# Two transposes of the first attention head leave TensorE for VectorE and a round trip through HBM

## The chip, the cores and the metric

The kernel runs on one core of one Trainium2 chip. The metric is the device time of one execution in microseconds (us). Before the change it is 1411.34 us, the median of three runs (1411.06 to 1411.61).

The core's engines each work through a queue of their own, in order: TensorE (PE; its weight loads are listed apart as PEld), VectorE (DVE), ScalarE (ACT), GpSimd (POOL), and SyncE (SP), which here only issues DMAs. An engine waits when the instruction at the head of its queue waits.

## The reference

Two layers, 512 tokens, width 1024, float32. Cut to what matters here:

```python
for i in range(DEPTH):                                   # 2
    xn = rmsnorm(x, norm1_g[i])
    u_pool, q, k, v, g_a, g_b = split(xn @ w_in[i])
    q, k = rotary(rmsnorm(q)), rotary(rmsnorm(k))        # 4 heads x 2 halves x 128
    p = softmax(where(chunk_causal, q @ k.T * scale, neg))
    a = p[:, :, 0] - lam * p[:, :, 1]                    # one probability matrix per head
    o = rmsnorm(a @ v, subln_g[i]) * (1.0 - lam_init)    # v: 256 wide per head
    merged = sigmoid(g_a) * pool_mixer(u_pool) + sigmoid(g_b) * o
    x = x + merged @ w_out[i]
    x = x + (silu(gate) * up) @ w_ffn_out[i]             # gate, up = split(rmsnorm(x) @ w_ffn_in[i])
```

## The kernel before, in words

Every float32 product is done as three products of rounded halves: `split` (L196) makes a high part on ACT (a cast) and a low part on DVE (a subtraction), and `product` (L277) issues high x high, high x low, low x high on PE. So a tile that PE is to use passes through ACT and DVE first, and its low part is the last to be ready.

The four heads are processed in the order 3, 2, 1, 0. Below, the first (number 3 of the first layer) is called A and the second B. Tokens are in four tiles t = 0 to 3 of 128. For each head `attention` (L549) does this:

- For each tile a product gives q and k (512 wide); ACT squares them with sums, DVE and POOL make the reciprocal root `r` (L328, L329), DVE scales (L659) and rotates (L431), and `qn` is the result. It is transposed, split into `qh`, `ql` (L198, L199) and used by `scores` (L569).
- `scores` computes two score tiles `sc` of (t+1) x 128 columns, takes the maximum on DVE, the exponential on ACT, and combines both halves into `prob[0]` on DVE (L587).
- The probabilities must be transposed before they can be multiplied with v. `turn_prob` (L595) splits the transposed tile into `ah` and `al`.
- `weighted` (L609) multiplies with v into a PSUM tile (`oy`, and for A's odd tiles one of the two score tiles `sc`), normalises and gates it on DVE into `m` (tile `mt`, L617 to L620).
- `turn_out` (L628) puts the transposed `m` into `mj`, which the merge of this head (`merged`, L724) adds much later.

A transpose is done in one of two ways. `transpose` (L302) is a PE instruction with an identity, 128x128, into PSUM. `turned` (L306) transposes 32x32 squares on DVE into `near` (L310), writes `near` to HBM (`away`, L311) and reads it back in four DMAs with the squares in their new places (L313); SP issues all five, and each read waits for the write to land. `near` shares its buffers with the tiles it is made from: `pr0`/`pr1` for probabilities, `mt` for outputs.

Before the change A uses PE for all its transposes (qn, probabilities, outputs), and so do the last head's outputs. All other heads' qn and probabilities, and the outputs of B and of the third head, go by `turned`.

The order of the work is set twice. The code keeps a clock of PE work (`clock`, counted in columns of a product, so one unit is about 0.44 us per thousand) and a list of steps due later (`later`, L263; `run_due`, L267): the delays of L47 and L49 say how much PE work lies between a step and the next. A step that `need` (L337) asks for is run early. A scheduler then places each instruction in its engine's queue by its own estimate of durations, so neighbouring steps can be interleaved.

Weights are loaded by SP into seven buffers (`raw`), in the order in which they are used, and split into six pairs (`whi`, `wlo`).

Of the kernel before, what the change touches and what calls it, by code (L numbers as in the profile page):

```python
# [18 lines left out]
P = 128  # L19
# [3 lines left out]
NT = S // P  # L23
# [19 lines left out]
ORDER = (3, 2, 1, 0)  # L43

HIDDEN_AT = {0: "u", 2: "m", 4: "pr", 6: "us", 8: "mj", 10: "u", 12: "m", 14: "pr", 16: "us", 18: "u", 20: "m"}

SCORE_WAIT, PROB_WAIT, AV_WAIT, NORM_WAIT, MERGE_WAIT = 33600, 25200, 11400, 15000, 15000  # L47

QK_AWAY, SCORE_AWAY, PROB_AWAY, MERGE_AWAY = 28000, 26000, 32000, 24000  # L49

# [59 lines left out]
def trunk_kernel(  # L110
# [21 lines left out]
    def s_ps():  # L132
        return ps.tile([P, 512], F32, name="sc", tag="sc", bufs=2)

    def tr_ps():
        return ps.tile([P, 512], F32, name="tr", tag="tr", bufs=2)
# [59 lines left out]
    def split(hi, lo, src):  # L196

        ins = nc.scalar.copy(hi, src)  # L198
        nc.vector.tensor_sub(lo, src, hi.bitcast(F32))  # L199
        return ins  # L200
# [62 lines left out]
    def later(delay, what):  # L263
        heapq.heappush(waiting, (clock[0] + delay, count[0], what))
        count[0] += 1
# [11 lines left out]
    def product(acc, pairs):  # L277

        n = len(pairs)
        for i, ((ah, al), (bh, bl)) in enumerate(pairs):  # L280
            run_due()
            nc.tensor.matmul(acc, lhsT=ah, rhs=bh, start=i == 0, stop=False)  # L282
            nc.tensor.matmul(acc, lhsT=ah, rhs=bl, start=False, stop=False)  # L283
            nc.tensor.matmul(acc, lhsT=al, rhs=bh, start=False, stop=i == n - 1)  # L284
            clock[0] += 3 * acc.shape[-1]
# [16 lines left out]
    def transpose(dst, src):  # L302
        nc.tensor.transpose(dst, src, ident)  # L303
        clock[0] += 2 * P

    def turned(src, n, tag, bufs):  # L306

        near = sb.tile([P, n * P], F32, name="near", tag=tag, bufs=bufs)
        away = hbm.tile([P, n * P], F32, name="away", tag="away", bufs=8)
        nc.vector.transpose(near.rearrange("p (c k j) -> p k c j", c=4, k=n), src.rearrange("p (k c i) -> p k c i", k=n, c=4))  # L310
        nc.sync.dma_start(away, near)  # L311
        for c in range(4):
            nc.sync.dma_start(  # L313
                near[32 * c:32 * (c + 1), :].rearrange("i (q r) -> i q r", q=4),
                away.rearrange("(q i) (c r) -> c i q r", q=4, c=4)[c])
        return near.rearrange("p (q k j) -> p k q j", q=4, k=n)

    def squares_of(x):
        return x.rearrange("p k (q j) -> p k q j", q=4)
# [12 lines left out]
    def small(name, width=1):  # L332
        return sb.tile([P, width], F32, name=name, tag=name, bufs=4)
# [109 lines left out]
    def token(t):  # L443
        return slice(t * P, (t + 1) * P)
# [90 lines left out]
    for layer in range(L):  # L535
# [13 lines left out]
        def attention(j, before, then):  # L549
# [9 lines left out]
            def turn(t, qn):  # L559
                if at_start:  # L560
                    tp = tr_ps()
                    for h in range(4):
                        transpose(tp[:, h * P:(h + 1) * P], qn[:, h, :])
                    split(qh[:, :, token(t)], ql[:, :, token(t)], tp.rearrange("p (h c) -> p h c", h=4))
                else:
                    split(squares_of(qh[:, :, token(t)]), squares_of(ql[:, :, token(t)]), qn)
                later(SCORE_WAIT if at_start else SCORE_AWAY, lambda: scores(t))

            def scores(t):  # L569
                width = (t + 1) * P  # L570
                prob = []
                st = small("st", 2)
                mx = small("mx", 2)
                for c in range(2):
                    sc = s_ps()
                    product(sc[:, :width], [(
                        (qh[:, c, token(t)], ql[:, c, token(t)]), (qh[:, 2 + c, :width], ql[:, 2 + c, :width]))])
                    nc.vector.memset(sc[:CHUNK, width - CHUNK:width], MASKED)
                    nc.vector.tensor_reduce(mx[:, c:c + 1], sc[:, :width], axis=AX.X, op=ALU.max, negate=True)
                    pr = sb.tile([P, S], F32, name="pr", tag=f"pr{c}", bufs=2)  # L580
                    nc.scalar.activation(pr[:, :width], sc[:, :width], AF.Exp, bias=mx[:, c:c + 1], accum_out=st[:, c:c + 1])
                    prob.append(pr[:, :width])
                rc = small("rc", 2)
                nc.vector.reciprocal(rc, st)
                nc.vector.tensor_mul(rc[:, 1:2], rc[:, 1:2], neglam[layer])
                nc.vector.tensor_scalar_mul(prob[1], prob[1], rc[:, 1:2])
                nc.vector.scalar_tensor_tensor(prob[0], prob[0], rc[:, 0:1], prob[1], op0=ALU.mult, op1=ALU.add)  # L587
                if at_start:
                    later(PROB_WAIT + (4000 if t == NT - 1 else 0), lambda: turn_prob(t, prob[0]))
                else:  # L590
                    near = turned(prob[0], t + 1, f"pr{t % 2}", 2)
                    later(PROB_AWAY, lambda: turn_prob(t, near))
                ready.add((layer, j, "s", t))

            def turn_prob(t, pr):  # L595
                if at_start:
                    tp = tr_ps()
                    for k in range(t + 1):
                        transpose(tp[:, token(k)], pr[:, token(k)])
                apart = at_start and t % 2  # L600
                ah, al = (sb.tile([P, S], F32R, name="a" + p, tag="u" if apart else "a" + p, bufs=2 if apart else 1) for p in "hl")
                width = (t + 1) * P
                if at_start:
                    split(ah[:, :width], al[:, :width], tp[:, :width])
                else:
                    split(*(squares_of(x[:, :width].rearrange("p (k c) -> p k c", c=P)) for x in (ah, al)), pr)
                later(AV_WAIT, lambda: weighted(t, ah, al))

            def weighted(t, ah, al):  # L609
                if (layer, j, "v", t) not in ready:  # L610
                    later(2400, lambda: weighted(t, ah, al))
                    return
                o = s_ps()[:, :VD] if at_start and t % 2 else o_ps()
                product(o, [((ah[:, token(k)], al[:, token(k)]), (v_at(vh, k), v_at(vl, k))) for k in range(t + 1)])
                ss = small("sso")
                m = sb.tile([P, VD], F32, name="mt", tag="mt", bufs=3)
                nc.scalar.activation(m, o, AF.Square, accum_out=ss)  # L617
                r = rsqrt_mean(ss, VD, 1, (1.0 - lam_init,))
                nc.vector.scalar_tensor_tensor(m, o, r, sg[layer], op0=ALU.mult, op1=ALU.mult)
                nc.vector.scalar_tensor_tensor(m, tb[t // 2][:, t % 2, :], 1.0, m, op0=ALU.add, op1=ALU.mult)  # L620
                ready.add((layer, j, "o", t))
                if near_end:
                    later(MERGE_WAIT, lambda: turn_out(t, m))
                else:
                    near = turned(m, 2, "mt", 3)
                    later(MERGE_AWAY, lambda: turn_out(t, near))
# [9 lines left out]
                ready.add((layer, j, "mj", t))  # L636

            at_start = not layer and j == ORDER[0]
            near_end = at_start or j == ORDER[-1]
            if not at_start:  # L640
                w = wblock(KD)
            for t in range(NT):
# [298 lines left out]
        for i, j in enumerate(ORDER):  # L941
            then = (lambda: project_out(ORDER[i - 2:i - 1], False)) if i >= 2 else None
            mjs[j] = attention(j, ORDER[i - 1] if i else None, then)
            if i:
                mix(i - 1)
# [102 lines left out]
```

## Time and profile before

| | us |
|---|---|
| median of 3 runs | 1411.34 |
| the profiled execution | 1411.17 |
| its span in the profile | 1409.4 |
| PE transposes of A's probabilities | 10, from 56.0 to 71.7 |
| PE transposes of A's outputs | 8, from 69.8 to 85.9 |

The page of the profile gives each engine's busy time and count, then the chain of work that ended last, followed back from the end. The view of waits says who waited for whom (us in total, times, longest). The view of stretches gives each engine's busy time between two moments. The timeline lists instructions with start, length, engine, line, tiles and the idle time ahead of them. All times are us from the start of the span.

### The profile page before, as it was taken

How to read it: one execution, taken by the hardware profiler on the slowest of the kernel's cores; microseconds unless marked ns; L12 is line 12 of the kernel's file. 1: busy time of each engine (PE TensorE's matmuls, PEld its weight loads, DVE VectorE, ACT ScalarE, POOL GpSimd, SP SyncE). 2: the span in 40 equal slices, each digit the busy share in tenths (PEclk: the TensorE clock that was granted, in tenths of full speed). 3: DMA queues.
4: the chain of work that ended last, by engine and by line, in shares of the span. 5: the costliest groups of instructions: out<-in, count | busy, mean ns of one | idle time of the engine just before them, and what ended most of it. 6: DMA issues, size and time to landing. Idle time of an engine off the chain costs nothing.

```text
span 1409.4 us, 21870 instructions
## 1 busy us (share of the span) xinstructions
PE 1403.4 (100%) x8156; PEld 1239.0 (88%) x8156; DVE 1023.0 (73%) x1915; ACT 686.8 (49%) x1309; POOL 118.2 (8%) x144
## 2 busy tenths in 40 slices
PE   9999999999999999999999999999999999999999
PEld 7888888888999899989888888888889998999897
DVE  7779787687998548737578787767769975676462
ACT  6554343443766346526354543435447662563350
POOL 1010000100001001000010101000010000010000
PEclk9999999999999999999999999999999999999999
DMA  9345353443278357629335355434424682685351
GB/s 363 104 130 148 121 164 108 141 147 84 75 180 208 111 132 183 190 49 235 120 115 170 117 168 166 142 112 154 145 45 120 161 231 73 150 185 160 99 141 60
DMA packets 104219, 201.11 MB, mean 143 GB/s; under 512 B 32688, under 2 KB 56752, under 8 KB 104112
## 3 DMA queue, kind: packets, MB, share of 16 engines
q1 hardware_dynamic: 94176, 166.14, 36.6%
q0 software_dynamic: 8640, 31.46, 12.6%
q10 hardware_dynamic: 1296, 2.11, 0.5%
q8 instruction: 64, 1.05, 0.3%
q14 instruction: 43, 0.35, 0.1%
HBM read 183.02 MB, written 16.65 MB: 142 GB/s over the span
## 4 chain that ended last, share of the span: by engine, by line
PE 95%; DVE 2%; DMA 1%; issue 0%; POOL 0%; ACT 0%; SPq 0%; DVEq 0%; POOLq 0%; ACTq 0%
PE mm L282 19%; PE mm L284 19%; PE mm L283 19%; PE mm L296 6%; PE mm L297 6%; PE mm L294 6%; PE sc L294 3%; PE sc L297 3%; PE sc L296 3%; PE tr L297 1%; PE tr L296 1%; PE tr L294 1%; PE tr L303 1%; PE sc L284 1%; PE sc L283 1%; PE sc L282 1%
## 5 line engine op out<-in xcount | busy, mean ns | idle before, releaser
L198 ACT CAST whi<-raw 128x1024 fp32r<-128x1024 f32 (+1 forms) x225 | 234.6, 1047 | 212.6 <-issue 92.9
L199 DVE TENSOR_TENSOR wlo<-raw,whi 128x1024 fp32r<-128x1024 f32 (+1 forms) x225 | 271.8, 1215 | 74.2 <-ACT whi L198 71.5
L282 PE MATMUL mm<-whi,xh 128*128 128x512 f32 x480 | 188.7, 393 | 0.0
L283 PE MATMUL mm<-wlo,xh 128*128 128x512 f32 x480 | 187.2, 390 | 0.0
L284 PE MATMUL mm<-whi,xl 128*128 128x512 f32 x480 | 187.2, 390 | 0.0
L761 DVE TENSOR_TENSOR res<-mm,res 128x512 f32<-128x512 f32 (+1 forms) x97 | 65.7, 682 | 113.2 <-PE mm L284 113.2
L284 PE MATMUL mm<-whi,fl 128*128 128x512 f32 (+1 forms) x358 | 138.5, 387 | 0.0
L282 PE MATMUL mm<-whi,fh 128*128 128x512 f32 (+1 forms) x358 | 138.3, 387 | 0.0
L283 PE MATMUL mm<-wlo,fh 128*128 128x512 f32 (+1 forms) x358 | 138.2, 387 | 0.0
L329 POOL TENSOR_TENSOR r<-r,mhalf 128x1 f32<-128x1 f32 (+1 forms) x76 | 63.8, 840 | 614.5 <-DVE r L328 493.5
L284 PEld LDWEIGHTS mm<-whi,xl 128*128 128x128 f32 x480 | 90.1, 188 | 19.2
L283 PEld LDWEIGHTS mm<-wlo,xh 128*128 128x128 f32 x480 | 90.3, 188 | 17.4
L282 PEld LDWEIGHTS mm<-whi,xh 128*128 128x128 f32 x480 | 90.2, 188 | 17.4
L238 POOL DMA_DIRECT2D wlo<-in_wts x60 | 52.6, 876 | 604.3 <-ACT wlo L237 290.4
L282 PE MATMUL mm<-xh,whi 128*128 128x512 f32 x256 | 100.4, 392 | 0.0
L283 PE MATMUL mm<-xl,whi 128*128 128x512 f32 x256 | 99.8, 390 | 0.0
L284 PE MATMUL mm<-xh,wlo 128*128 128x512 f32 x256 | 99.8, 390 | 0.0
L296 PE MATMUL mm<-xql,whi 128*128 128x256 f32 x352 | 99.7, 283 | 0.0
L294 PE MATMUL mm<-xqh,whi 128*128 128x256 f32 x352 | 99.6, 283 | 0.0
L297 PE MATMUL mm<-xqh,wlo 128*128 128x256 f32 x352 | 99.6, 283 | 0.0
L294 PE MATMUL sc<-xqh,whi 128*128 128x256 f32 x320 | 90.7, 283 | 0.0
L294 PE MATMUL mm<-xrh,whi 128*128 128x256 f32 x320 | 90.6, 283 | 0.0
(243 smaller groups left out, 3512.1 us busy)
## 6 DMA issues: line engine op xcount, KB each, us to landing
raw<-in_wts SPq DMA_DIRECT2D x244, 512.0 KB, 4.3
wlo<-in_wts POOLq DMA_DIRECT2D x60, 512.0 KB, 7.6
away<-near SPq DMA_DIRECT2D x35, 256.0 KB, 2.4
near<-away SPq DMA_DIRECT2D x140, 64.0 KB, 2.1
away<-near SPq DMA_DIRECT2D x27, 128.0 KB, 1.8
near<-away SPq DMA_DIRECT2D x108, 32.0 KB, 2.3
xr<-in_x_t SPq DMA_DIRECT2D x4, 512.0 KB, 7.0
res<-in_x SPq DMA_DIRECT2D x4, 512.0 KB, 9.0
```

The costliest lines, as they stand in the source:

```text
L198: ins = nc.scalar.copy(hi, src)
L199: nc.vector.tensor_sub(lo, src, hi.bitcast(F32))
L238: nc.gpsimd.dma_start(lo.rearrange("p a b -> p (a b)"), wts[piece_no], accum_op=ALU.add)
L282: nc.tensor.matmul(acc, lhsT=ah, rhs=bh, start=i == 0, stop=False)
L283: nc.tensor.matmul(acc, lhsT=ah, rhs=bl, start=False, stop=False)
L284: nc.tensor.matmul(acc, lhsT=al, rhs=bh, start=False, stop=i == n - 1)
L294: nc.tensor.matmul(acc[:, i, :], lhsT=ah, rhs=bh, start=start and not i and not k, stop=False, skip_group_check=True)
L296: nc.tensor.matmul(acc[:, i, :], lhsT=ah, rhs=bl, start=False, stop=False, skip_group_check=True)
L297: last = nc.tensor.matmul(acc[:, i, :], lhsT=al, rhs=bh, start=False, stop=i == 1 and k == 3, skip_group_check=True)
L303: nc.tensor.transpose(dst, src, ident)
L329: nc.gpsimd.tensor_tensor(r, r, mhalf[:, :width], op=ALU.pow)
L761: added = nc.vector.tensor_add(res[t][:, cs], here, res[t][:, cs])
```

## The change

A's probabilities and outputs now go by `turned`, like those of B. Only its q and k are still transposed by PE. The delay `PROB_WAIT` falls away: for A the step from probabilities to `turn_prob` is now 32000 units (`PROB_AWAY`) instead of 25200 (29200 for the last tile), and from `m` to `turn_out` 24000 (`MERGE_AWAY`) instead of 15000.

```diff
-SCORE_WAIT, PROB_WAIT, AV_WAIT, NORM_WAIT, MERGE_WAIT = 33600, 25200, 11400, 15000, 15000
+SCORE_WAIT, AV_WAIT, NORM_WAIT, MERGE_WAIT = 33600, 11400, 15000, 15000
...
-                if at_start:
-                    later(PROB_WAIT + (4000 if t == NT - 1 else 0), lambda: turn_prob(t, prob[0]))
-                else:
-                    near = turned(prob[0], t + 1, f"pr{t % 2}", 2)
-                    later(PROB_AWAY, lambda: turn_prob(t, near))
+                near = turned(prob[0], t + 1, f"pr{t % 2}", 2)
+                later(PROB_AWAY, lambda: turn_prob(t, near))
...
             def turn_prob(t, pr):
-                if at_start:
-                    tp = tr_ps()
-                    for k in range(t + 1):
-                        transpose(tp[:, token(k)], pr[:, token(k)])
...
-                if at_start:
-                    split(ah[:, :width], al[:, :width], tp[:, :width])
-                else:
-                    split(*(squares_of(x[:, :width].rearrange("p (k c) -> p k c", c=P)) for x in (ah, al)), pr)
+                split(*(squares_of(x[:, :width].rearrange("p (k c) -> p k c", c=P)) for x in (ah, al)), pr)
...
-            near_end = at_start or j == ORDER[-1]
+            near_end = j == ORDER[-1]
```

What this moves in the queues is seen in three places. (Lines from 588 on are ten lower in the changed kernel, and the number behind a tile's name tells the instances of one program apart; `xh`, `xl` are the input's halves.)

PE, where A's last tile is weighted. Before, `mm_849` is B's third q/k product, `mt_807` an output tile of A, `sc_903` the weighted sum of A's fourth tile with `ah_858`, `al_859`:

```order
L282 MATMUL mm_849<-whi_694,xh_118 128x512
L283 MATMUL mm_849<-wlo_695,xh_118 128x512
L284 MATMUL mm_849<-whi_694,xl_119 128x512
L303 MATMUL tr_899<-ident_68,mt_807 128x128 x2
L282 MATMUL sc_903<-vh_381,ah_858 128x256
L283 MATMUL sc_903<-vl_382,ah_858 128x256
L284 MATMUL sc_903<-vh_381,al_859 128x256
```

Now `mm_942` is B's fourth q/k product (the third, `mm_857`, has ended ahead of it), `sc_976` the weighted sum of A's fourth tile with `ah_877`, `al_878`:

```order
L282 MATMUL mm_942<-whi_712,xh_118 128x512
L283 MATMUL mm_942<-wlo_713,xh_118 128x512
L284 MATMUL mm_942<-whi_712,xl_119 128x512
L282 MATMUL mm_942<-whi_718,xh_118 128x512
L282 MATMUL sc_976<-vh_381,ah_877 128x256
L283 MATMUL sc_976<-vl_382,ah_877 128x256
L283 MATMUL mm_942<-wlo_719,xh_118 128x512
L284 MATMUL mm_942<-whi_718,xl_119 128x512
L284 MATMUL sc_976<-vh_381,al_878 128x256
```

The sum has moved from inside B's third product into its fourth, and the transposes around it are gone.

DVE, around the low part of the same tile. Before, `r_827` and `qn_821` belong to B's second tile, `mt_807` to A's second output:

```order
L328 TENSOR_SCALAR r_809<-sso_806 128x1
L619 SCALAR_TENSOR_TENSOR mt_807<-sc_799,r_809,hg_234 128x256
L620 SCALAR_TENSOR_TENSOR mt_807<-tb_383,mt_807 128x256
L328 TENSOR_SCALAR r_827<-ss4_822,stats_70 128x2 x2
L659 SCALAR_TENSOR_TENSOR qn_821<-mm_762,r_827,hg_234 128x128 x4
L199 TENSOR_TENSOR al_859<-tr_853,ah_858 128x512
```

Now `qn_829` belongs to B's second tile, `mt_889` to A's second output, `r_920` and `qn_914` to B's third tile, `wlo_1072` to weights that B needs later:

```order
L328 TENSOR_SCALAR r_891<-sso_888 128x1
L310 STREAM_TRANSPOSE near_849<-qn_829 128x4x4x32
L609 SCALAR_TENSOR_TENSOR mt_889<-sc_881,r_891,hg_234 128x256
L610 SCALAR_TENSOR_TENSOR mt_889<-tb_383,mt_889 128x256
L310 STREAM_TRANSPOSE near_896<-mt_889 128x2x4x32
L328 TENSOR_SCALAR r_920<-ss4_915,stats_70 128x2 x2
L649 SCALAR_TENSOR_TENSOR qn_914<-mm_857,r_920,hg_234 128x128 x4
L199 TENSOR_TENSOR wlo_1072<-raw_1069,whi_1071 128x1024
L199 TENSOR_TENSOR al_878<-near_693,ah_877 128x512
```

The low part has moved behind the third tile's `r` and `qn` and behind a weight split.

SP, from A's first trip on. Before, thirteen weight loads stand in a row here and the trips of B's q and k follow them:

```order
L212 DMA raw<-in_wts 128x1024 x9
L311 DMA away<-near 128x128
L313 DMA near<-away 32x4x32 x4
L212 DMA raw<-in_wts 128x1024 x3
L311 DMA away<-near 128x256
L313 DMA near<-away 32x4x64 x4
L311 DMA away<-near 128x384
L212 DMA raw<-in_wts 128x1024
L313 DMA near<-away 32x4x96 x4
```

The trips of A's probabilities (128 to 512 wide) now stand between the weight loads; further on, up to four writes stand ahead of the first read. Past A's and B's stretch the queues hold the same instructions in the same order on PE.

## The prediction

> **What bounds the kernel now.** I read the page from the busy times to the chain that ended last, then the waits of TensorE, then the stretches in which the first two heads run.
>
> ```profile
> PE 1403.4 (100%) x8156; PEld 1239.0 (88%) x8156; DVE 1023.0 (73%) x1915; ACT 686.8 (49%) x1309; POOL 118.2 (8%) x144
> PE 95%; DVE 2%; DMA 1%; issue 0%; POOL 0%; ACT 0%; SPq 0%; DVEq 0%; POOLq 0%; ACTq 0%
> PE mm L456 <- DVE cold L449: 1.2, 1, 1.2
> PE oy L284 <- DVE al L199: 0.5, 2, 0.4
> PE tr L512 <- DVE xh L499: 0.4, 1, 0.4
> PE oy L282 <- ACT ah L198: 0.2, 1, 0.2
> ```
>
> TensorE (PE) is busy without a gap, it makes 95% of the chain, and in the whole span it waits 2.3 us for anybody (the four rows of its waits: total, times, longest). So an instruction taken off PE is worth what it holds PE for, and any wait put on PE costs its full length.
>
> ```profile
> 60.00:75.00 15.00, 15.00 (x81) 12.64 (x80) 10.65 (x35) 6.55 (x29) 3.58 (x4) 1.00 0.23 79
> 75.00:90.00 15.00, 15.00 (x79) 12.63 (x79) 12.07 (x33) 9.28 (x29) 2.12 (x4) 1.00 0.36 111
> 105.00:120.00 15.00, 15.00 (x72) 12.64 (x71) 13.96 (x30) 8.67 (x20) 0.55 (x1) 1.00 0.50 151
> 120.00:135.00 15.00, 14.62 (x75) 12.32 (x73) 14.01 (x40) 5.95 (x12) 1.92 (x2) 1.00 0.35 104
> ```
>
> The columns of these stretches are PE, weight load, VectorE (DVE), ACT, POOL, granted clock, DMA share, GB/s. The clock is full. DVE is the engine behind PE: 11 to 12 of 15 us busy where the first head (A) hands over to the second (B), 14 of 15 us in B's stretch, where PE already waits 0.4 us for a DVE result (`al`, in 120 to 135).
>
> **What goes.** Ten transposes of A's probabilities (1+2+3+4) and eight of its outputs (4 tiles of 2).
>
> ```profile
> L303 PE MATMUL tr<-ident,pr x10: 270/271/273, 56.0 to 71.7; 128*128 128x128 f32 x10
> L303 PE MATMUL tr<-ident,mt x8: 271/272/273, 69.8 to 85.9; 128*128 128x128 f32 x8
> 71.12 0.39 PE L284 MATMUL mm<-whi,xl 128*128 128x512 f32 x1
> 71.35 0.60 PE L303 MATMUL tr<-ident,pr 128*128 128x128 f32 x4
> 71.70 0.47 PE L282 MATMUL mm<-whi,xh 128*128 128x512 f32 x1
> 72.02 0.39 PE L283 MATMUL mm<-wlo,xh 128*128 128x512 f32 x1
> ```
>
> One lasts 0.27 us but they overlap, so the price is read from starts. Between the start of the four and the second product behind them lie 72.02 - 71.35 = 0.67 us; the product alone takes 0.23 (71.12 to 71.35). Four cost 0.44, one 0.11. Eighteen: **-1.98 us**. [...] The trace shows 0.27 as the length of one and 0.11 as its distance to the next, and PE pays the distance.
>
> **What comes.** Eight DVE square transposes, eight writes to HBM and 32 reads back, all issued by SP, and longer delays before the work that needs them.
>
> ```profile
> L310 DVE STREAM_TRANSPOSE near<-pr x4: 313/506/709, 96.6 to 120.6; 128x128 f32<-128x128 f32 x1, 128x256 f32<-128x256 f32 x1, 128x384 f32<-128x384 f32 x1, 128x512 f32<-128x512 f32 x1
> L310 DVE STREAM_TRANSPOSE near<-mt x4: 435/438/439, 114.1 to 138.3; 128x256 f32<-128x256 f32 x4
> 71.03 0.33 SPq L311 DMA_DIRECT2D away<-near  x1
> 73.06 2.02 SPq L313 DMA_DIRECT2D near<-away  x4
> near<-away SPq DMA_DIRECT2D x4, 64.0 KB, 2.1
> near<-away SPq DMA_DIRECT2D x4, 16.0 KB, 2.0
> ```
>
> Head B has the same four shapes now, so every piece has a price: on DVE 4 x 0.51 for the probabilities and 4 x 0.44 for the outputs, 3.8 us by durations (about 3.2 by starts), spread over 49 to 96 us. On SP one trip is 2.0 us from the write to the first read, 2.0 of issuing, and 2.1 (last two rows, by size) to the last landing: about 6.2 us. Cover for DVE: it idles 4.4 and 2.9 us in the stretches 60 to 75 and 75 to 90. None of this is on the chain by itself.
>
> The reads of A's narrow tiles come in pieces of 128 or 256 bytes. [...] In the rows above the 16 KB reads of B's first tile, in pieces of 128 bytes, land as soon as the 64 KB ones. Were they twice as slow, the first tile would be some 2 us later and cost PE under 1 us by the next paragraph.
>
> Past which queue work is moved: on SP the 13 weight loads in a row are cut after the ninth by the first trip.
>
> ```profile
> 52.59 0.33 SPq L212 DMA_DIRECT2D raw<-in_wts  x1
> 85.26 1.05 ACT L198 CAST whi<-raw 128x1024 fp32r<-128x1024 f32 x1 [0.20 <-PE mm L284]
> ```
>
> The tenth of these loads is issued at 52.59 and its cast is at 85.26. Counted in order it is the eighth cast from 50 us on. A load that starts 4 us later is still some 25 us early, so I cost this at nothing; were that cover gone, it would cost the whole delay.
>
> First tile of A: its weighted sum now needs a trip instead of one transpose. Its softmax ends on DVE at 49.46 (first row below), the transpose at 49.8, and the trip of 6.2 us, less a little for a small write, lands near 55.5. Behind its cast (0.3) ACT has a weight cast (1.05) and a tanh (0.5), up to 57.3, and then the exponential on which the fourth tile's scores wait:
>
> ```profile
> 49.11 0.35 DVE L587 SCALAR_TENSOR_TENSOR pr<-pr,rc 128x128 f32<-128x128 f32 x1
> 57.92 0.58 ACT L581 ACTIVATE pr<-sc,mx 128x384 f32<-128x384 f32 x1 [0.23 <-DVE mx L579]
> 58.65 0.50 PE L282 MATMUL sc<-qh 128*128 128x512 f32 x1
> ```
>
> The exponential runs about 0.4 later (DVE has one more transpose ahead), PE comes there 0.5 later as well, since three more products stand ahead. Bounds: 0 to 0.8 us of wait; I take 0.
>
> **The wait I expect: A's fourth tile.** In the new order of DVE its low part `al` stands behind B's third tile (r, qn) and a weight split; before it stood behind B's second tile.
>
> ```profile
> 72.62 0.35 DVE L328 TENSOR_SCALAR r<-ss,stats 128x2 f32<-128x2 f32 x2
> 74.17 1.13 DVE L659 SCALAR_TENSOR_TENSOR qn<-mm,r,hg 128x128 f32<-128x128 f32 x4 [1.20 <-POOL r L329]
> 75.22 0.68 DVE L199 TENSOR_TENSOR al<-tr,ah 128x512 fp32r<-128x512 f32 x1
> 77.00 0.38 PE L303 MATMUL tr<-ident,mt 128*128 128x128 f32 x2
> 77.13 0.36 PE L282 MATMUL sc<-vh,ah 128*128 128x256 f32 x1
> 78.64 0.40 PE L282 MATMUL mm<-whi,xh 128*128 128x512 f32 x1
> 79.53 0.28 ACT L655 ACTIVATE qn<-mm 128x128 f32<-128x128 f32 x1 [0.22 <-PE mm L284]
> 80.46 0.22 ACT L655 ACTIVATION_READ_ACCUMULATOR qn<-mm 128x1 f32 x1
> 81.64 0.35 DVE L328 TENSOR_SCALAR r<-ss,stats 128x2 f32<-128x2 f32 x2
> 83.18 1.13 DVE L659 SCALAR_TENSOR_TENSOR qn<-mm,r,hg 128x128 f32<-128x128 f32 x4 [1.19 <-POOL r L329]
> 84.23 1.22 DVE L199 TENSOR_TENSOR wlo<-raw,whi 128x1024 fp32r<-128x1024 f32 x1
> 85.36 0.29 DVE L436 TENSOR_TENSOR m<-qn,tab 128x128 f32<-128x128 f32 x1
> ```
>
> Now `al` is done near 75.8 and PE needs it near 77.4. Afterwards: B's third product ends on PE at 79.31 before (0.22 ahead of ACT's square). Ahead of it go away ten probability transposes (1.12 with 0.02 of switching), four of the outputs (0.44), and the weighted sums of A's third and fourth tile, which move behind it (12 products from 77.13 to 78.64 are 1.51, nine 1.1): 75.1. From there PE runs 6 products of B's fourth tile (1.37), the third weighted sum (1.08), 7 more products (1.60), two of the fourth sum (0.24), two more (0.46), and wants `al` at **79.9**. DVE: ACT's four squares end 0.22 + 1.15 behind 75.1, so r can start at 76.5; but ahead of it stand two transposes and the first half of an output tile. Laid end to end from the second tile's qn (PE gives its product near 68.8) they free DVE at 76.9. Then r to qn 1.55 (rows, twice), qn 1.05, the weight split 1.13, `al` 0.6: **81.3**. PE waits **1.4 us**. If DVE is free when r is ready it is 0.8; if POOL or the trips make DVE 0.9 later it is 2.2. I keep 0.7 and 2.2 as ends.
>
> **What follows in B.** Everything behind that wait shifts with PE. In B's stretch DVE has one us in 15 free, and its order there is new too.
>
> ```profile
> 132.31 0.65 DVE L199 TENSOR_TENSOR al<-near,ah 128x512 fp32r<-128x512 f32 x1
> ```
>
> Laying DVE's rows end to end from B's scores I get `al` of B's four tiles between 0.4 and 0.6 us before PE wants them, the last at about 137.3 against 137.7. The old wait of 0.4 (for the row above) may go or stay; I count nothing for it, with ends of -0.4 and +2. Later heads keep their order.
>
> **Sum** against the profiled execution's 1411.17 us (span 1409.4 and 1.8 around it; the median is 0.17 higher, less than this sum can tell): 1411.17 - 1.98 + 1.4 = **1410.6 us**.
>
> **Rivals.**
> 1. *The gain arrives whole.* `al` would have to be done by 79.9, so DVE would have to reach B's third tile before its squares end and the weight split would have to overlap. For it: the waits of before are tiny. Against it: r to `al` alone is 4.3 us behind a product that PE ends 4.75 us before its need, with 1.4 of squares between. Time 1411.17 - 1.98 = 1409.2, with the old wait gone 1408.8.
> 2. *Slower: DVE becomes the bound in B.* Place: 105 to 140 us. There DVE is 28 of 30 us busy; the 3.2 us of new transposes must be absorbed before, in the 7.3 us it idles between 60 and 90. Those idles are waits for POOL and ACT in the middle of chains, so perhaps they can't be filled. If none is absorbed, and SP's trips, of which up to four writes now stand ahead of the first read, add one more landing of 2.1, PE waits 1.4 + 3.2 + 2.1: 1411.17 - 1.98 + 6.7 = 1415.9. It decides once DVE is over 0.5 late in B, and makes the kernel measurably slower from 4.8 us of waits in all. Half of it gives 1412.5.
> 3. *The change doesn't take PE's work away.* The order lists no such transposes for A any more; nothing speaks for it.
>
> **How the numbers follow.** This kernel's measurement can tell about 0.2%, 2.8 us, from no change. Forecast (wait 0.7 to 2.2): 0.50. Rival 1: 0.20, no change by that bound. Half of rival 2, up to 1414: 0.15. Rival 2 in full: 0.12. More than 2.8 us faster needs a gain that I can't find on PE: 0.03. So faster 0.03, same 0.85, slower 0.12. The range leaves out rival 2 in full and the tip of rival 1: 1408.9 to 1413.6.
>
> **What would show it.** PE with 18 transposes fewer; a new PE wait of 0.7 to 2.2 us for `al` near 80 us (a weighted sum in the scores' buffer); no PE wait for weights; trips of 6 to 7 us. Wrong would be: no wait there (rival 1), waits of several us between 100 and 140 us for `al`, `ql` or `ul` (rival 2), or a wait for the exponentials near 59 us.

## The result and the profile after

| | before | after |
|---|---|---|
| median of 22 runs, us | 1411.39 | 1413.7 |
| lowest to highest | 1410.85 to 1412.17 | 1412.83 to 1415.39 |
| the profiled execution, us | 1411.17 | 1413.29 |
| its span | 1409.4 | 1411.5 |

The ratio is 1.0016 with a 95% interval of 1.001 to 1.0023: the changed kernel is 2.3 us slower, where 0.6 us faster was forecast. Two single runs of experiments 6 and 9 with a far lower granted clock (0.66 and 0.89; 1976 and 2679 us) are left out of every figure below. The page's busy times and the first line of its chain, after:

```profile
PE 1403.0 (99%) x8138; PEld 1236.9 (88%) x8138; DVE 1025.0 (73%) x1923; ACT 686.5 (49%) x1309; POOL 117.4 (8%) x144
PE 93%; DVE 3%; DMA 2%; SPq 1%; issue 1%; ACT 0%; POOL 0%; DVEq 0%; ACTq 0%; POOLq 0%
```

The 18 transposes are gone from PE (8156 to 8138) and eight are new on DVE (1915 to 1923). The chain now leaves PE for DMA, DVE and SP. The waits of PE over the whole span (total, times, longest), after:

```profile
PE sc L284 <- DVE al L199: 1.7, 1, 1.7
PE mm L456 <- DVE cold L449: 1.2, 1, 1.2
PE oy L284 <- DVE al L199: 1.1, 2, 0.7
PE sc L282 <- ACT pr L581: 0.6, 1, 0.6
PE oy L282 <- ACT ah L198: 0.2, 1, 0.2
PE sc L282 <- ACT ah L198: 0.2, 1, 0.2
```

2.3 us of waits became 5.0. Three rows are new, the first, the fourth and the sixth; the third grew from 0.5, and a wait of 0.4 for `xh` is gone. The stretches in which the large ones of A and B lie, after:

```profile
75.00:90.00 15.00, 13.10 (x67) 10.64 (x66) 12.81 (x30) 7.20 (x19) 3.71 (x4) 1.00 0.39 117
90.00:105.00 15.00, 14.36 (x71) 12.03 (x70) 10.40 (x37) 6.08 (x23) 1.01 (x1) 1.00 0.41 131
105.00:120.00 15.00, 15.00 (x69) 12.32 (x68) 11.53 (x24) 9.66 (x21) 0.54 (x1) 1.00 0.31 85
120.00:135.00 15.00, 15.00 (x74) 12.57 (x74) 14.50 (x40) 5.27 (x13) 1.32 (x2) 1.00 0.58 183
```

PE has holes of 1.9 us in 75 to 90 and 0.6 in 90 to 105, and none from 105 to 135; the hole of 0.4 that stood in the last row before is gone.

**A's fourth tile, near 82 us.** SP, ACT, DVE and PE of the changed kernel (the two SP rows first, with the number of DMAs; then ACT; then DVE; then PE):

```profile
69.09 2.94 SPq L311 DMA_DIRECT2D away<-near  x3
72.14 6.91 SPq L313 DMA_DIRECT2D near<-away  x12
76.44 0.28 ACT L645 ACTIVATE qn<-mm 128x128 f32<-128x128 f32 x1 [2.74 <-DVE near L310]
78.77 0.64 ACT L198 CAST ah<-near 128x512 fp32r<-128x512 f32 x1
77.37 0.45 DVE L310 STREAM_TRANSPOSE near<-mt 128x256 f32<-128x256 f32 x1
77.74 0.32 DVE L328 TENSOR_SCALAR r<-ss,stats 128x2 f32<-128x2 f32 x2
79.26 1.13 DVE L649 SCALAR_TENSOR_TENSOR qn<-mm,r,hg 128x128 f32<-128x128 f32 x4 [1.20 <-POOL r L329]
80.30 1.22 DVE L199 TENSOR_TENSOR wlo<-raw,whi 128x1024 fp32r<-128x1024 f32 x1
81.43 0.69 DVE L199 TENSOR_TENSOR al<-near,ah 128x512 fp32r<-128x512 f32 x1
79.46 0.39 PE L282 MATMUL sc<-vh,ah 128*128 128x256 f32 x1 [0.16 <-ACT ah L198]
80.03 0.40 PE L284 MATMUL mm<-whi,xl 128*128 128x512 f32 x1
82.17 0.38 PE L284 MATMUL sc<-vh,al 128*128 128x256 f32 x1 [1.74 <-DVE al L199]
```

This is the forecast wait, in the forecast place, with the forecast line in front of it (r, qn, a weight split, `al`). PE could have gone on at 80.03 + 0.23 = 80.26 and went on at 82.17, so 1.91 us are lost here; with the small wait for `ah` ahead of it about 2.2. The trip was not what held it up. Its write was issued at 69.09, and the last of its four reads (the first four of the twelve) was issued at 73.53 and took 3.1 us, so the data had landed near 76.6, after 7.5 us where 6 to 7 were forecast. `ah` was cast 2.2 us later, because ACT had the squares of B's third tile, a weight cast and an output's square ahead of it without a gap. Those squares had begun only at 76.44, though PE had finished their product near 75.1: by the profile, DVE's transpose of B's second tile released them. So ACT's line put off `ah`, and the late squares put off r as well as DVE's own line did (they ended near 77.6, r began at 77.74).

**B's second tile of scores, near 97 us.** DVE, then PE:

```profile
96.17 0.71 DVE L310 STREAM_TRANSPOSE near<-qn 128x512 f32<-128x512 f32 x1
96.81 0.25 DVE L579 TENSOR_REDUCE mx<-sc 128x1 f32<-128x128 f32 x1
97.60 0.39 PE L282 MATMUL sc<-qh 128*128 128x256 f32 x1 [0.64 <-ACT pr L581]
```

There are two score tiles. The second one comes free only when ACT has taken the exponential of what it held before, for which DVE must find the maximum, and DVE is late: it gets to this maximum at 96.81, behind a transpose, though PE had made those scores by 91.8. The prediction had looked for B's waits at `al`, not here.

**The third head, near 216 us.** The same product in the trace of before and, in the second fence, of after:

```profile
214.03 0.40 PE L283 MATMUL mm<-xl,whi 128*128 128x512 f32 x1
214.58 0.38 PE L284 MATMUL oy<-vh,al 128*128 128x256 f32 x1
```

```profile
216.45 0.38 PE L284 MATMUL oy<-vh,al 128*128 128x256 f32 x1 [0.73 <-DVE al L199]
```

The product ahead of it starts at 215.32, so PE loses 0.90 us here, where it lost 0.32 before.

How the loss adds up is read from PE's own position. The first product of A's merge and the first one that reads `fh`, before and then after:

```profile
145.21 0.39 PE L282 MATMUL mm<-whi,mh 128*128 128x512 f32 x1
466.06 0.40 PE L282 MATMUL mm<-whi,fh 128*128 128x512 f32 x1
```

```profile
146.14 0.39 PE L282 MATMUL mm<-whi,mh 128*128 128x512 f32 x1
467.94 0.40 PE L282 MATMUL mm<-whi,fh 128*128 128x512 f32 x1
```

By the end of B the change has cost 0.93 us net of its gain, by 466 us 1.88, and the span ends 2.1 later. So about half of the net loss arises behind both heads that the change touches (0.7 to 1.1 us between these two products in the six profiles of the changed kernel).

### The profile page after: what moved, and what is told of

The parts are those of the page before. It is cut to its first block, busy times and chain, and to the rows that moved or that the text cites. A ratio compares the mean times of both kernels' runs of the same rounds, so it can differ in the third digit from the quotient of the medians.

```text
span 1411.5 us, 21911 instructions
## 1 busy us (share of the span) xinstructions
PE 1403.0 (99%) x8138; PEld 1236.9 (88%) x8138; DVE 1025.0 (73%) x1923; ACT 686.5 (49%) x1309; POOL 117.4 (8%) x144
## 4 chain that ended last, share of the span: by engine, by line
PE 93%; DVE 3%; DMA 2%; SPq 1%; issue 1%; ACT 0%; POOL 0%; DVEq 0%; ACTq 0%; POOLq 0%
PE mm L283 18%; PE mm L282 18%; PE mm L284 18%; PE mm L296 6%; PE mm L294 6%; PE mm L297 6%; PE sc L294 3%; PE sc L297 3%; PE sc L296 3%; PE tr L297 1%; PE tr L296 1%; PE tr L294 1%; DMA near<-away 1%; PE tr L303 1%; SPq L313 1%
```

## The experiments

The times of the kernel before, taken alongside, are 1411.19 for experiments 1 to 4, 1411.10 for 5 to 8 and 1411.21 for 9. The theory at the start: the wait near 82 us is the largest loss, the third head's the second. The rivals: the gain was never there; the loss belongs to the outputs' half; or DVE is late as a whole and any wait that is taken away comes back at its next customer.

**1. What a transpose on PE is worth.** The kernel before, each of the 18 transposes issued twice:

```
 transpose(tp[:, token(k)], pr[:, token(k)])
+nc.tensor.transpose(tp[:, token(k)], pr[:, token(k)], ident)
...
+nc.tensor.transpose(tp[:, a * P:(a + 1) * P], m[:, a * P:(a + 1) * P], ident)
```

> The kernel before, with each of the 18 transposes of the first head's probabilities and outputs issued twice in a row on TensorE; the second writes the same place with the same values, and nothing else is changed. It prices one transpose in place. Theory A (the prediction's price, 0.11 us each, the start-to-start spacing): 18 x 0.11 = 2.0 us slower than before, near 1413.4 us. Rival B (the rows' duration counts, 0.27 each): 4.9 us slower, near 1416.3. Rival C (TensorE's time there is not on the path): no change, 1411.4.

Measured 1412.94 (1412.71 to 1413.34) against 1411.19: +1.75 us, 0.10 for one. Theory A. PE pays the distance between starts, not the 0.27 us that a row shows, and the gain forecast was right within 0.23 us.

**2. The weighted sum of the fourth tile later.** The changed kernel with

```
-later(AV_WAIT, lambda: weighted(t, ah, al))
+later(AV_WAIT + (8000 if at_start and t == NT - 1 else 0), lambda: weighted(t, ah, al))
```

> The changed kernel, with the weighted sum of the first head's fourth tile due 8000 later in the planner's units, so that TensorE takes it up behind the second head's fourth projection and not in the middle of it. VectorE's order ahead of `al` stays. Theory A (most of the loss is the wait for `al` of the fourth tile near 82 us, 2.4 us by start spacings): that wait goes, and the time is 1.8 to 2.6 us below the changed kernel's, near 1411.5. Rival B (the wait only moves to the next place where VectorE is late, the second head's scores or its `al`): the wait near 82 goes and the waits behind it grow by as much, 1413.7. Rival C (the loss comes from SP's order of weight loads and trips in the third head): the time falls by the wait near 82 at most and the third head keeps its wait of 0.7 us near 216.

Measured 1413.4 (1412.21 to 1414.72). The wait for `al` near 82 is gone, and this stands in the waits of 54 to 146 us:

```profile
PE sc L282 <- DVE mt L609: 2.1, 1, 2.1
```

The sum uses one of the two score tiles, and B's scores now wait for DVE to empty it. Rival B; the wait in the third head stays too (0.8), as rival C had it.

**3 and 4. Each half alone.** The outputs alone are the kernel before with the first pair of lines, the probabilities alone the changed kernel with the second:

```
-near_end = at_start or j == ORDER[-1]
+near_end = j == ORDER[-1]
...
-near_end = j == ORDER[-1]
+near_end = at_start or j == ORDER[-1]
```

> Half of the change: the first head's four output tiles go by VectorE's squares and the trip through HBM, its probabilities stay on TensorE (8 transposes fewer than before, not 18). Theory A (the cost is that `al` of the fourth tile stands behind a longer line on VectorE and a trip, so it belongs to the probabilities): 8 x 0.11 = 0.9 us faster than before, 1410.5, and no TensorE wait for `al` near 80 us. Rival B (SP's order in the third head costs about 0.9 and comes with the outputs' trips): no change against before, 1411.4, with a wait of 0.7 near 216. Rival C (VectorE's time as such costs): slower than before by about a quarter of the changed kernel's loss, 1412.

> The other half: the first head's probabilities go by VectorE's squares and the trip, its four output tiles stay on TensorE (10 transposes fewer than before). Theory A (the cost belongs to the probabilities): a TensorE wait for `al` of the fourth tile of 0.5 to 2 us near 80, and 10 x 0.11 = 1.1 us gained against it: between 1411.0 and 1413. Rival B (the cost belongs to the outputs' trips): no wait for `al` near 80 and 1.1 us faster than before, 1410.3.

Outputs alone: 1412.72 (1411.89 to 1413.71), +1.5 us. Probabilities alone: 1411.73 (1411.49 to 1412.54), +0.5, inside what can be told from no change. (The profile of the latter is of its slowest run.) Together 2.0, near the whole. The wait for `al` does belong to the probabilities, as the waits of that run between 54 and 146 us have it:

```profile
PE sc L284 <- DVE al L199: 1.3, 1, 1.3
```

but ten transposes saved (1.0) pay for most of it. The outputs' half costs more although it has no such wait (0.4 us for an earlier tile, 0.6 in the third head). Of that run's theories C comes nearest in the time, but the wait of 0.6 near 216 is the one that rival B named. PE shows where the loss lies: at A's merge this kernel stands at 145.30 against 145.21, its gain used up, at the first `fh` product at 466.66 against 466.06, and its span is 1.4 us longer. So nearly all of its net loss lies behind B.

**5 and 6. The outputs' half taken apart.** The kernel before, with PE's transposes left in, plus either the four square transposes on DVE, whose result nothing reads, or the four trips, whose result nothing reads; both into tiles of the buffers `mt` that the change uses, and both for A alone (`if at_start`, left out below).

```
+near = sb.tile([P, VD], F32, name="near", tag="mt", bufs=3)
+nc.vector.transpose(near.rearrange("p (c k j) -> p k c j", c=4, k=2), m.rearrange("p (k c i) -> p k c i", k=2, c=4))
```

```
+scr = sb.tile([P, VD], F32, name="near", tag="mt", bufs=3)
+away = hbm.tile([P, VD], F32, name="away", tag="away", bufs=8)
+nc.sync.dma_start(away, m)
+for c in range(4):
+    nc.sync.dma_start(
+        scr[32 * c:32 * (c + 1), :].rearrange("i (q r) -> i q r", q=4),
+        away.rearrange("(q i) (c r) -> c i q r", q=4, c=4)[c])
```

> The kernel before, plus the four square transposes of the first head's output tiles on VectorE, into a tile from the outputs' own buffers that nothing reads; no trip is made, TensorE still transposes. It adds 4 x 0.45 = 1.8 us of VectorE alone. Theory A (VectorE's time and place in line cost): TensorE's waits for `al` and for the score buffers grow, 0.5 to 1.5 us slower than before, 1411.7 to 1412.7. Rival B (the loss of the outputs' half comes from the trips on SP): no change, 1411.2.

> The kernel before, plus the four trips of the first head's output tiles through HBM (one write, four reads each) into tiles of the outputs' buffers that nothing reads; no square transposes on VectorE, TensorE still transposes, so nothing waits for what the trips bring. Theory A (VectorE is the cost): no change, 1411.2. Rival B (the trips push other trips and weight loads back on SP, also in later heads): 1 to 2.4 us slower than before, 1412.2 to 1413.6, with a wider spread of the single times as in the outputs-only kernel (1411.89 to 1413.71).

DVE's part: 1411.88, +0.8, which can't be told from no change (1411.5 to 1413.0; five of the eleven times are 1412.4 or more). The trips' part: 1414.57, +3.5, with nobody waiting for what they bring. This is two groups of times: four runs with a clock of 1.0 at 1413.0 (+1.9, in the range of rival B) and six with a clock of 0.998 or 0.999 at 1414.5 to 1414.9 (experiment 10 tells of this clock). Rival B holds in the price, not in the mechanism: the third head loses only 0.2 us here. In the kernel with the trips, four reads on SP and the square on ACT that needs an `mt` tile, and then PE's waits between 80 and 100 us:

```profile
82.38 1.77 SPq L627 DMA_DIRECT2D near<-away  x4
86.10 0.37 ACT L617 ACTIVATE mt<-sc 128x256 f32<-128x256 f32 x1
```

```profile
PE tr L303 <- DVE mt L620: 0.8, 1, 0.8
PE sc L282 <- DVE mt L619: 0.7, 1, 0.7
```

Before, that square ran as soon as PE had its product:

```profile
78.84 0.38 ACT L617 ACTIVATE mt<-sc 128x256 f32<-128x256 f32 x1 [0.54 <-PE sc L284]
```

There are three `mt` tiles, a trip holds one until its reads have landed (the last of the four shown, issued near 83.8, near 85.8 by an estimate from the 2.0 us that reads of 32 KB took before), and the fourth output cannot leave its score tile; on ACT its square now stands behind four weight casts, the last of which ends as it begins. In the changed kernel the same square is late too (85.95), but B's scores start at 90.97, behind the wait near 82, and no longer meet it.

**7 and 8. The fourth tile of probabilities back on PE**, once with the outputs' trips (14 transposes fewer than before) and once without (6 fewer): the branch of before, with `if at_start and t == NT - 1`.

> The changed kernel with one exception: the first head's fourth tile of probabilities is transposed by TensorE as before (4 transposes come back, 14 stay away, all four output tiles still make the trip). Theory A (the largest loss is the wait for `al` of the fourth tile near 82 us): that wait goes, 2.4 us less and 4 x 0.1 more, 1411.7. Rival B (the outputs' half carries the loss, as its own run of 1412.7 says): the time stays between 1412.3 and 1413.3 although the wait near 82 is gone, because other waits stay.

> The first three tiles of probabilities of the first head by VectorE and the trip, the fourth tile and all four output tiles by TensorE as before: 6 transposes fewer. Theory A (latency and line of the fourth tile were the cost of the probabilities' half): no TensorE wait above 0.5 us for `al` near 80, and 6 x 0.1 = 0.6 us faster than before, 1410.6, so faster than both kernels. Rival B (VectorE's added time moves the waits into the second head): 1411.2 or slower.

With the trips 1413.07 (1411.98 to 1415.38), without 1412.48 (1411.72 to 1413.66). The wait near 82 is gone in both, and others stand in its place; the first two rows are of the one with the trips (54 to 230 us), the last two of the other (54 to 146):

```profile
PE sc L282 <- ACT pr L581: 1.6, 3, 0.6
PE oy L284 <- DVE al L199: 0.8, 1, 0.8
```

```profile
PE tr L303 <- DVE mt L620: 0.8, 1, 0.8
PE oy L284 <- DVE up L706: 0.3, 1, 0.3
```

Rival B both times: the waits are now for the exponentials ahead of B's scores, for the outputs' transposes, for later `al` and DVE's `up`. No version of the study beats the kernel before.

**9. The price of such a wait by itself.** The kernel before, `al` of the fourth tile computed four times more:

```
+for _ in range(4 if t == NT - 1 else 0):
+    nc.vector.tensor_sub(al[:, :width], tp[:, :width], ah[:, :width].bitcast(F32))
```

> The kernel before, with the low part `al` of the first head's fourth tile computed five times in a row on VectorE instead of once (the same values into the same place); no transposes move and no trip is added. By the rows of before, four more of 0.6 us and what the order puts between them end near 79.8 us; TensorE wants it near 78.3, so a wait of about 1.5 us at the changed kernel's place, made by VectorE alone. Theory A (such a wait costs its length and about 0.3 more, and below some 1.7 us the clock stays): 1.5 to 1.9 us slower than before, 1412.6 to 1413.0, clock 1.0 in all runs. Rival B (slack behind it in the second head takes it up): within 0.5 us of before. Rival C (a single wait of this size already drops the clock): a second group of times 1.5 us higher, with a mean clock of 0.998 to 0.999.

1412.89 against 1411.21, +1.7, with a clock of 1.0 in all ten runs. But the times form two groups: six from 1412.58 to 1412.98, as Theory A has it, and four from 1413.87 to 1414.12. The row in the profile, which is of the lower group:

```profile
79.81 0.39 PE L284 MATMUL sc<-vh,al 128*128 128x256 f32 x1 [1.20 <-DVE al L606]
```

At A's merge PE stands at 146.77 against 145.21 (146.59 in a second profile, experiment 11): a wait that is reported as 1.2 us holds PE up by 1.4 to 1.6. Theory A for the lower group; B's stretch gives nothing back. The upper group is 1.2 us longer at full clock, so it is not rival C either, and what makes it was not found.

**10. The changed kernel profiled again.** In 13 of its 22 runs the mean granted clock is 1.0 and the time 1412.8 to 1413.9; in 9 it is 0.998 or 0.999 and the time 1413.8 to 1415.4. Five more profiles, for the place:

> The changed kernel itself, one look. In 9 of its 22 timed runs the mean clock was 0.998 or 0.999 and the time 1413.8 to 1415.4; in the others 1.0 and 1412.8 to 1413.9. Theory A (the clock drops for about 4 us behind the wait near 82 us): a look with a clock below 1.0 shows products of 512 columns 0.43 us apart in place of 0.23 just behind that wait, and nowhere else. Rival B (the long runs have longer waits in the third head, and a lower clock is a by-product there): the 0.43 spacing, if any, stands near 200 to 217 us.

> The changed kernel itself, a fourth look. Theory A (the clock drops behind the wait near 82 us): if the mean clock of this run is below 1.0, products of 512 columns stand 0.43 us apart in place of 0.23 for some 4 us just behind that wait, and the time is 1413.8 or more. Rival B: the low clock stands in the third head, behind a longer wait there. With a clock of 1.0 the run tells nothing on this and the time is 1412.8 to 1413.9.

> The changed kernel itself, a second look, for the same question as the first; beside it, whether the third head's wait for `al` near 216 us (0.7 us in the first profile) is there in every run, or only where the reads of two trips near 184 us take over 4.4 us on SP, as the profiles so far have it (3.7 to 3.9 us without a loss, 4.5 to 5.4 with one).

> The changed kernel itself, a third look, for the same two questions as the second.

> The changed kernel itself, a fifth look, for the same question as the fourth.

All five have the waits of the first profile: 1.7 to 1.8 us near 82 and 0.7 to 0.8 near 216. Four had a clock of 1.0 (1412.84 to 1413.43), the fourth 0.998 and 1414.17. PE there, and then its stretches, with the clock in the third column from the right:

```profile
82.11 0.38 PE L284 MATMUL sc<-vh,al 128*128 128x256 f32 x1 [1.75 <-DVE al L199]
83.40 0.62 PE L282 MATMUL mm<-whi,xh 128*128 128x512 f32 x1
83.81 0.63 PE L283 MATMUL mm<-wlo,xh 128*128 128x512 f32 x1
...
86.80 0.41 PE L284 MATMUL mm<-whi,xl 128*128 128x512 f32 x1
87.05 0.40 PE L282 MATMUL mm<-whi,xh 128*128 128x512 f32 x1
```

```profile
80.00:85.00 5.00, 3.25 (x16) 2.60 (x15) 4.52 (x12) 0.68 (x3) 1.60 (x1) 0.84 0.75 247
85.00:90.00 5.00, 5.00 (x19) 3.96 (x18) 3.72 (x6) 2.93 (x5) 0.55 (x1) 0.82 0.16 37
```

Theory A: from 1.3 us behind the wait on (82.11 to 83.40) eight products take 0.43 us each in place of 0.23, for 3.4 us. That is 1.6 us. DVE uses them to catch up, so the 0.8 us lost near 97 shrink to 0.2 and about 1.0 is left; the medians of the two groups of times differ by 0.84 (1413.33 and 1414.17).

**11. The third head.** The times of experiments 5 and 9 each have a lower and an upper group, all at a clock of 1.0. Their kernels were profiled once more, to see whether the third head makes the difference:

> The kernel before with the four square transposes of the output tiles added on VectorE, once more. Theory A (the upper group of its times is the third head's loss): with a time of 1411.5 to 1411.9 there is no TensorE wait of 0.5 us near 199 us and none of 0.8 near 216, the weight load issued near 183.5 us lands in under 4 us (5.5 in the first profile), and the eight reads behind it take under 4 us on SP (5.3 in the first). Rival B (the upper group is lost elsewhere): the waits near 199 and 216 are there in a run of the lower group too.

> The kernel before with `al` of the fourth tile computed five times, once more. Theory A (its upper group of times is the third head's loss): with a time near 1414 there are TensorE waits of 0.5 to 0.8 us near 200 and 217 us that the first profile (lower group) does not have, and the weight load near 184.6 us takes over 4.4 us to land (3.9 in the first). Rival B: the upper group is lost elsewhere, for example at the second layer's waits for `al` near 781 and 915 us.

The first came out at 1411.95, near its lower group (its first profile, at 1413.03, is of the upper one), and has neither the wait near 199 nor one of 0.8 near 216: theory A there. The second came out at 1412.83, in the lower group once more, so what makes the upper group of experiment 9 stays open. But the profiles together order themselves. Five things per profile, in us: the landing of the weight load that SP issues between 183 and 186, and when within it a block of instructions is fetched by DMA (behind the load's issue); the time SP needs for the eight reads of two trips right behind it; how long ACT then idles for the reads that bring the first probabilities (`ah`, 128x128); and PE's wait for `al` near 216.

| kernel | load lands in | fetch begins | eight reads | ACT idles | PE waits |
|---|---|---|---|---|---|
| before | 3.6 | none | 3.72 | 1.7 | none |
| all 18 doubled | 3.7 | none | 3.72 | 1.8 | none |
| `al` five times | 3.9 | 0.6 | 3.73 | 2.0 | none |
| probabilities alone | 3.5 | 0.8 | 3.69 | 1.9 | 0.2 |
| outputs' trips added | 3.7 | none | 3.72 | 1.8 | 0.2 |
| three tiles by DVE | 3.8 | 3.4 | 3.89 | 2.3 | 0.3 |
| outputs on DVE added, second profile | 4.2 | 1.5 | 4.07 | 2.4 | 0.3 |
| `al` five times, second profile | 4.5 | 1.2 | 4.47 | 2.6 | 0.5 |
| outputs alone | 4.5 | 1.2 | 4.47 | 2.7 | 0.6 |
| changed kernel, six profiles | 4.7 to 5.0 | 0.6 to 1.5 | 4.67 to 5.04 | 3.0 to 3.4 | 0.7 to 0.8 |
| fourth sum later | 4.9 | 0.6 | 5.36 | 2.9 | 0.8 |
| outputs on DVE added | 5.5 | 0.3 | 5.31 | 3.6 | 0.8 |
| fourth tile on PE, with trips | 4.1 | 1.1 | 3.82 | 2.9 | 0.8 |

SP's reads and ACT's cast, before and then after:

```profile
183.57 3.72 SPq L313 DMA_DIRECT2D near<-away  x8
187.51 0.30 ACT L198 CAST ah<-near 128x128 fp32r<-128x128 f32 x1 [1.73 <-DMA near<-away]
```

```profile
184.75 4.80 SPq L313 DMA_DIRECT2D near<-away  x8
189.87 0.30 ACT L198 CAST ah<-near 128x128 fp32r<-128x128 f32 x1 [3.13 <-DMA near<-away]
```

The wait grows with ACT's idle time through the whole table, to within about 0.2 us. The reads bring the third head's q, k and first probabilities and stand behind the load on SP's queue. Behind the cast on ACT stands the exponential of the next scores, behind that DVE's whole line up to `al`, and that chain has no slack. In the changed kernel the slow load is there in every profile.

What slows the load can in part be read from the DMA view. After the change it has this row from 181.5 to 186.5 us, and before it has none there:

```profile
q8 instruction: 1, 0.02, 1.3%
```

This is a block of 16 KB; the whole trace has 64 of them, one for about 254 instructions of PE (8138 products and as many weight loads). That they are PE's own code is the author's inference from this count; the row names no engine. Before, the block was fetched from 181.1 us on, 2.0 ahead of the load; after, from 185.7 on, 1.5 behind its issue. Both come at nearly the same count of PE instructions, 1687 and 1683: with 36 fewer of them ahead (18 transposes and their weight loads), the same count falls later in the work. In the first profile of the changed kernel the load's last five packets of 4 KB end one by one, 0.16 us apart, the last of them 4.25 us behind the issue; before, the last packet ends at 3.2. That is 1.0 us later, and the fetch took 1.06; what held the five packets back is not shown. Every load of 4.1 us or more has a fetch, of this or of a second kind of 8 KB, in its first 1.5 us; but two loads with a fetch there took only 3.5 and 3.9, and no run moved the fetch alone. So a collision of the load with the fetch is likely, not shown. SP's order is a weaker rival: the changed kernel is one weight load behind at that point (the 34th of L212 there and the 35th before), but the kernel with DVE's work alone had the slow load with SP's order unchanged around it.

## Why the prediction was wrong

Terms in us, in the order of the prediction's sum. "Lost" is the distance from one PE start to the next, less the usual distance for that shape, from the first profile of each kernel:

| step of the prediction | said | measured |
|---|---|---|
| 18 transposes off PE | -1.98 | -1.75 (experiment 1) |
| scores near 59 us | 0 (0 to 0.8) | +0.1 |
| wait for `al` of A's fourth tile | +1.4 (0.7 to 2.2) | +1.9, and +0.3 for `ah` ahead of it |
| B's stretch | 0 (-0.4 to 2) | +0.5 |
| "Later heads keep their order" | no term | +0.95 up to 466 us, +0.2 behind |
| the clock | no term | about +0.8 in 9 of 22 runs |

Without the last row these make +2.2, and the two profiled executions differ by 1413.29 - 1411.17 = 2.1. The clock lifts the median of the 22 runs by a further 0.4 (1413.7 against 1413.33 for those without a drop).

- *The gain* was right, and so was reading it from starts.
- *The wait at A's fourth tile* was right in place and mechanism and too small by 0.8. But for the 0.3 us that it lost for `ah`, PE came there when the sum said (80.26, where 79.9 was said). The low part was late: r began at 77.74 in place of 76.9, and `al` was done near 82.1, not at 81.3. Two terms were short. DVE had a whole output tile ahead of r, as the order already listed, and not only "the first half" of one. And ACT's squares, counted from the end of the product (75.1), began at 76.44, because DVE's transpose of the tile before had to release them; so even a free DVE could not have begun r at 76.5. The sum's lower case of 0.8 comes to 0.9 by its own rows (76.5 + 4.33 - 79.9). The end of 2.2 had been kept for lateness of this kind.
- *B's stretch* was inside its ends, with the wrong place. No `al` of B made PE wait, as laid out, and the old wait of 0.54 went. The loss is 0.79 us at the second score tile near 97, and 0.24 near 137, where a weight load of PE waits for `ul`:

```profile
137.52 0.19 PEld L283 LDWEIGHTS mm<-ul,pwh 128*128 128x128 f32 x1 [0.38 <-DVE ul L199]
```

- *Rival 2*, DVE as the bound from 105 to 140 us, happened only by these 0.24 us: DVE is 11.53 of 15 us busy from 105 to 120, and PE has no hole there. The measured time lies in the stretch that the prediction gave to half of this rival (up to 1414), but that is chance, since most of the loss lies elsewhere. DVE was late earlier, from 77 to 98.
- ***"Later heads keep their order"* is the step that failed.** PE's order did stay, and so no term was set against it. But the third head's trips lie behind weight loads on the one queue of SP, and the room behind them was not priced. The trace of before has none: PE could have taken `al` at 214.03 + 0.23 = 214.26 and took it at 214.58. In its place the runs showed a wait for the first probabilities that is 1.4 us longer on ACT (1.73 to 3.13) and 0.95 us lost by PE up to 466 us: 0.58 more at `al` near 216, 0.27 at the scores near 199.5, the rest in smaller pieces. This costs as much as the net loss up to the end of B. Why the load ahead of those reads became slow is only made likely, by the fetch of instructions.
- *The trips* were costed at nothing because no one in A was in a hurry. They also hold `mt` tiles and stand in SP's way; the experiments with halves put the outputs, which the prediction hardly spoke of, at 1.5 of the 2 us.
- *The idle time of DVE* (7.3 us in 60 to 90) was taken as cover. Experiments 2, 7 and 8 speak against it: each removed the wait near 82, and each time waits behind DVE's line stood in its place.

## What to carry to other kernels

On a kernel whose busiest engine has no gaps, the idle time of the next engine need not be free: if it lies between steps of chains (here waits of 1.2 us for the root on POOL), extra work there can come out as a wait somewhere, and here curing one such wait (1.7 us for `al`) moved it (2.1 us for `mt`, experiment 2). When work is moved onto a shared queue, follow that queue through the stages behind, up to the next place where the trace shows a result taken the moment it is ready. Buffers that a slower path holds longer belong in the sum too, for the writers that wait for them (0.7 and 0.8 us for `mt` in experiment 6) as well as for the readers.

## What the runs showed of the chip

- In one profile of the changed kernel (experiment 10) a wait of PE of 1.75 us that ended at 82.11 was followed by 3.4 us (83.40 to 86.80) in which products of 512 columns start 0.43 us apart in place of 0.23. The granted clock is 0.84 from 80 to 85 us and 0.82 from 85 to 90, which is about half clock for the 3.4 us by an estimate from these two; from 70 to 80 and from 90 to 105 it is 1.0. The other five profiles of this kernel have a wait of 1.7 to 1.8 us there too, and a clock of 1.0. With the outputs' trips added, waits of 0.68 and 0.83 us, which end at 88.79 and 90.05, were followed by products 0.42 to 0.47 us apart from 90.36 on, with a granted clock of 0.66 from 90 to 95. A mean clock of 0.998 or 0.999 stands in 9 of 22 runs of the changed kernel, in 6 of 10 with the outputs' trips added, and in 5 of 11 with the fourth sum later (a wait of 2.1), of which none was profiled. With a longest wait of 1.2 or 1.3 us (experiments 4 and 9) it stands in none of 21. In 2 of 11 runs of the outputs alone the clock was 0.999 too, though its profile has no wait above 0.6 in A, B or the third head; where it dropped there was not seen. Why the clock drops in some runs and not in others is not shown.
- PE lost more at a wait than the row reports: 1.91 us for 1.74 near 82, 0.79 for 0.64 near 97 and 0.90 for 0.73 near 216 in the changed kernel, and 1.4 to 1.6 for 1.20 in experiment 9.
- The traces of both kernels have 64 blocks of 16 KB that come by DMA on q8, a queue of the kind `instruction`; in the changed kernel that is one for about 254 of PE's 8138 products and as many weight loads. With 36 of these instructions fewer ahead of it, the block that was fetched 2.0 us ahead of a weight load (from 181.1) came 1.5 us behind its issue (from 185.7).
